# Token-major projections in blocks of 512 columns instead of 256

## The chip, the core and the metric

One core of a Trainium2 chip. The metric is device microseconds of one execution, from which a median over runs is taken. The engines that matter are TensorE (matmul, and transposes as matmuls against an identity), VectorE, ScalarE, GpSimd, and SyncE, which issues most DMA transfers. The profile calls them PE, DVE, ACT, POOL and SP.

## What is computed

Two transformer blocks on 256 tokens of width 1024, in float32. The first block is a gated FFN, a mixer of two attentions (low-rank with rope, and dilated), and a second FFN; the second block works on its output and on a context that the first block's stream also feeds, with three mixers (mLSTM scan, differential attention, state-space scan), a gated merge and a convolutional FFN.

```python
def hybrid_mixer(u, ...):
    proj = u @ w_in
    cq, ckv, kr, dq, dk, dv, g = jnp.split(proj, ...)
    q = (rms_norm(cq, q_norm_g) @ w_uq)
    c_kv = rms_norm(ckv, kv_norm_g)
    ...
    merged = gates[:, :, 0] * (o_a @ w_branch_a) + gates[:, :, 1] * (o_b @ w_branch_b)
    return merged @ w_out

def first_block(x, positions, ...):
    f1 = swiglu(rms_norm(h, ffn1_pre_g), ffn1_w_gate, ffn1_w_up, ffn1_w_down)
    h = h + 0.5 * rms_norm(f1, ffn1_post_g)
    mix = hybrid_mixer(rms_norm(h, mix_pre_g), ...)
    h = h + rms_norm(mix, mix_post_g)
    f2 = swiglu(rms_norm(h, ffn2_pre_g), ...)
    return h + 0.5 * rms_norm(f2, ffn2_post_g)
```

## The kernel before

**Layout and precision.** The 256 tokens are two blocks of 128 (TB = 2). A product in float32 is made of three matmuls on rounded halves (`mm3`, L353 to L358): high by high, high by low, low by high. Activations that feed a projection stand transposed, as eight k-rows of 128 features by 256 tokens, each in a high and a low half (`Split`). A feature-major projection (`proj_fm`, L370) has the weights stationary and 256 tokens moving. A token-major one (`proj_tm`, L380) has 128 tokens stationary and the weight columns moving, and it is this kind that the change is about: blocks of 256 columns (224 for `w_in_a`), one PSUM tile of one bank for both token blocks, outer loop over the token blocks, inner loop over the eight k-rows. `down` (L390) is token-major too, with 512 columns moving and four accumulators.

**The order of the work.** The kernel sets the order of instructions by hand. The engines take what is queued for them in program order and meet through semaphores. `tick(us)` (L197) is called after each stretch of TensorE work with an estimate of its length. It advances a clock of the program (a number at build time, no time of the chip), then steps the side chains that are marked first (evacuations, made by `later`), then calls `weights.ahead()`, then steps each other side chain that is due, once. A side chain is a generator: what stands between two of its yields is queued in one go, and a yield can name a wait in the program's clock. `join` runs a side chain to its end at once.

**Weights.** `Weights` (L94) streams all weights in the order of use, in loads of 512 KB: `load` issues the DMA on SyncE's queue, five raw tiles deep (NRAW). `split` (L116) makes the high half on ScalarE (L127) and the low half on VectorE (L128) into a ring of four (RING). With 256 columns a load holds four k-rows, so a block has two loads; with 512 it holds two k-rows, so a block has four; with 336 three, three and two. `take` (L143), at the head of a block, splits what of the block isn't split yet, and sets `now` to the block's first load. `ahead` (L138) splits on while fewer than four loads in the ring have a number of `now` or above; so the loads of a block count as used when the next block is taken.

**The stages that use `proj_tm`.** `ctx_attn` (L1206), run beside the residual norm behind the first FFN; `mixer1` (L756) for `w_in_a` and `w_in_b`; `ctx_mlstm` (L1225), beside the residual norm behind the first mixer; `mixer2` (L1473) for the mLSTM values and output gate, and for query, key and value of the differential attention. `residual_norm` (L445) is a side chain whose steps go from PSUM through VectorE (L457, L460, L478) to `to_T`, eight transposes for a token block (L512). `low_rank` (L740) normalises two slices of `w_in_a`'s result (L747) and transposes them (L752). `lat_scalars` (L1303) makes the gate scalars of the mLSTM and ends in transposes (L1348). `prep_a` (L1521), the query and key chain of the differential attention, is started inside the loop over six blocks, at the fifth.

**Modulation rows.** `mod_rows` (L940) multiplies 16 pieces of a matrix, loaded on ScalarE's queue (L972), on VectorE (L980), and adds them up over partitions on TensorE (L957). Each of its passes has 22 steps, and it is due by the program's clock at a fixed pace: 6.0 us a step for two passes during the first mixer and later, 2.0 us for four more (88 steps) that start at the first tick when the two are done. What of the four is left when the second FFN ends is run at the join there, with no other work beside it.

Of the kernel before, what the change touches and what calls it, by code (L numbers as in the profile page):

```python
# [16 lines left out]
D = 1024  # L17
# [18 lines left out]
SHAPES = {"f1_gu": (8, 256), "f1_dn": (2, D), "w_in_a": (8, 224), "w_in_b": (8, 256), "w_in_g": (8, 256), "w_uq_t": (3, 384),  # L36
          "w_ukv": (2, 1024), "w_br_a": (4, 256), "w_br_b": (4, 256), "w_out_t": (2, D), "f2_gu": (8, 256), "f2_dn": (2, D),
          "w_ctx": (8, 256), "w_rows": (8, 32), "w_lat": (8, 256), "w_br_m2": (4, 256), "w_br_a2": (4, 256),
# [3 lines left out]
def weight_order():  # L42
# [8 lines left out]
    add("w_ctx", 4, 5, 6, 7)  # L51
    add("w_in_a", 0, 1, 2)
    add("w_rows", 0)
    add("w_in_b", 4, 5, 0, 1)
    add("w_uq_t", 0, 1)
    add("w_ukv", 0)
    add("w_in_b", 2, 3)
# [5 lines left out]
    add("w_ctx", 2, 3, 0, 1)  # L63
    add("f2_gu", *range(NFF))
    add("f2_dn", *range(NFF // 2))
    add("w_ctx", 8, 9, 10)
    add("w_rows", 0)
    add("w_lat", *range(24))
    add("w_br_m2", 0, 1, 2, 3)
    add("w_lat", 24, 25, 26, 27)  # L70
    add("w_br_a2", 0, 1, 2, 3)
    add("w_lat", 28, 29, 30, 31)
# [110 lines left out]
class Net:  # L183
# [196 lines left out]
    def proj_tm(self, name, i, xT, ps):  # L380

        nk, cols = SHAPES[name]
        w = self.weights.take(name, i)
        p = ps([128, TB, cols])
        for tb in range(TB):
            self.tm_block(p[:, tb], w, xT, nk, tb, 0, cols)
            self.tick(nk * 0.327)
        return p
# [367 lines left out]
    def mixer1(self, xT, m):  # L756
# [449 lines left out]
    def ctx_attn(self, xT):  # L1206
# [18 lines left out]
    def ctx_mlstm(self, xT):  # L1225
# [39 lines left out]
    def ctx_ssd(self, xT):  # L1265
# [3 lines left out]
        for i in range(3):  # L1269
            p = self.proj_fm("w_ctx", 8 + i, xT, self.psA)  # L1270
# [202 lines left out]
    def mixer2(self, xT, aside):  # L1473
# [11 lines left out]
        def evac(p, i):  # L1485
            for tb in range(TB):
                nc.scalar.activation(va[tb][:, 2 * i:2 * i + 2, :128], p[:, tb].rearrange("p (h d) -> p h d", h=2), AF.Copy)

        for i in range(2):
            s2 = self.later(0, evac, self.proj_tm("w_lat", 4 + i, xT, B), i)  # L1490
# [4 lines left out]
        def evac(p, i):  # L1495
# [5 lines left out]
        for i in range(2):  # L1501
            s3 = self.later(0, evac, self.proj_tm("w_lat", 6 + i, xT, B), i)
# [105 lines left out]
        def evac(p, i):  # L1608
            nc.scalar.activation((qa, ka, vv)[i // 2][:, :, (i % 2) * 256:(i % 2) * 256 + 256], p, AF.Copy)
# [312 lines left out]
```

## Time and profile before

| | us |
|---|---|
| median of three runs | 1292.15 |
| lowest, highest | 1290.20, 1292.22 |
| the profiled execution | 1290.56 |
| its span, first to last instruction | 1288.8 |

The profile shows one execution. Its span is cut into 40 slices on the page, with the busy share of each engine in tenths and the TensorE clock that was granted; it has groups of instructions by source line, with the mean duration of one and the idle time before them, and who ended that. The trace behind it can be asked for single instructions (start, duration, engine, line, operation, operands, and in brackets how long the engine stood idle before and whose result ended that) and for the busy time in windows. A matmul's duration there reaches past the start of the next, since matmuls are pipelined: what one costs is read from start to start.

### The profile page before, as it was taken

How to read it: one execution, taken by the hardware profiler on the slowest of the kernel's cores; microseconds unless marked ns; L12 is line 12 of the kernel's file. 1: busy time of each engine (PE TensorE's matmuls, PEld its weight loads, DVE VectorE, ACT ScalarE, POOL GpSimd, SP SyncE). 2: the span in 40 equal slices, each digit the busy share in tenths (PEclk: the TensorE clock that was granted, in tenths of full speed). 3: DMA queues.
4: the chain of work that ended last, by engine and by line, in shares of the span. 5: the costliest groups of instructions: out<-in, count | busy, mean ns of one | idle time of the engine just before them, and what ended most of it. 6: DMA issues, size and time to landing. Idle time of an engine off the chain costs nothing. (4 is left out here: it accounts for less than half of the span.)

```text
span 1288.8 us, 22199 instructions
## 1 busy us (share of the span) xinstructions
PE 1199.3 (93%) x8728; PEld 1115.0 (87%) x8728; DVE 934.0 (72%) x1603; ACT 624.1 (48%) x1063; POOL 66.9 (5%) x84
## 2 busy tenths in 40 slices
PE   7999998999999999999981699999999998999998
PEld 7999977999878889999860599999888897999977
DVE  4897857667766786767857878589666767888854
ACT  4454545455564464444420454556465344555542
POOL 0020000100000000000000001035100000000000
PEclk8999999999999999999995799999999998999999
DMA  7878785666343766657896355345413265555562
GB/s 265 273 229 256 257 291 195 206 218 218 123 135 116 292 199 221 222 188 247 299 338 216 100 195 190 133 156 172 143 54 100 98 209 216 172 173 181 179 241 85
DMA packets 80605, 251.32 MB, mean 195 GB/s; under 512 B 9523, under 2 KB 10851, under 8 KB 80502
## 3 DMA queue, kind: packets, MB, share of 16 engines
q1 hardware_dynamic: 61654, 215.85, 49.6%
q10 hardware_dynamic: 18432, 33.56, 7.8%
q0 software_dynamic: 416, 0.50, 0.4%
q8 instruction: 68, 1.11, 0.3%
q14 instruction: 35, 0.29, 0.1%
HBM read 241.46 MB, written 8.42 MB: 194 GB/s over the span
## 5 line engine op out<-in xcount | busy, mean ns | idle before, releaser
L128 DVE TENSOR_TENSOR wl<-raw,wh 128x1024 fp32r<-128x1024 f32 (+3 forms) x358 | 424.1, 1218 | 137.0 <-ACT wh L127 133.8
L356 PE MATMUL pB<-u,wh 128*128 128x256 f32 x1696 | 486.6, 287 | 0.7 <-ACT u L347 0.7
L358 PE MATMUL pB<-u,wl 128*128 128x256 f32 x1696 | 481.9, 284 | 1.0 <-DVE wl L128 1.0
L357 PE MATMUL pB<-u,wh 128*128 128x256 f32 x1696 | 481.5, 284 | 0.6 <-DVE u L348 0.3
L127 ACT ACTIVATE wh<-raw 128x1024 fp32r<-128x1024 f32 (+3 forms) x358 | 359.3, 1045 | 93.1 <-PE pB L358 33.8
L356 PEld LDWEIGHTS pB<-u,wh 128*128 128x128 f32 x1696 | 326.0, 192 | 9.4 <-issue 6.8
L358 PEld LDWEIGHTS pB<-u,wl 128*128 128x128 f32 x1696 | 326.0, 192 | 2.3 <-DVE wl L128 1.4
L357 PEld LDWEIGHTS pB<-u,wh 128*128 128x128 f32 x1696 | 326.0, 192 | 1.8 <-DVE u L348 1.4
L356 PE MATMUL pB<-wh,u 128*128 128x512 f32 (+3 forms) x614 | 208.1, 339 | 1.7 <-ACT wh L127 1.7
L357 PE MATMUL pB<-wl,u 128*128 128x512 f32 (+3 forms) x614 | 207.6, 338 | 2.2 <-DVE wl L128 2.0
L358 PE MATMUL pB<-wh,u 128*128 128x512 f32 (+3 forms) x614 | 206.5, 336 | 0.0
L357 PEld LDWEIGHTS pB<-wl,u 128*128 128x128 f32 x614 | 117.0, 191 | 15.7 <-DVE wl L128 5.0
L356 PEld LDWEIGHTS pB<-wh,u 128*128 128x128 f32 x614 | 117.0, 191 | 14.1 <-ACT wh L127 2.4
L358 PEld LDWEIGHTS pB<-wh,u 128*128 128x128 f32 x614 | 117.0, 190 | 11.7
L428 POOL TENSOR_TENSOR rs<-ms,nhalf 128x1 f32<-128x1 f32 (+2 forms) x30 | 28.4, 946 | 877.2 <-DVE ms L422 874.5
L520 ACT ACTIVATE w<-pB 128x256 f32<-128x256 f32 x44 | 16.9, 383 | 116.7 <-PE pB L358 116.3
L980 DVE SCALAR_TENSOR_TENSOR v<-v,silu_c,v 128x512 f32<-128x512 f32 x84 | 62.8, 748 | 12.3 <-DMA v<-w_mod 11.2
L1006 DVE SCALAR_TENSOR_TENSOR w<-pB,cols,w 128x255 f32<-128x255 f32 x120 | 49.6, 476 | 15.8 <-ACT w L1001 10.1
L521 DVE SCALAR_TENSOR_TENSOR w<-w,pB 128x256 f32<-128x256 f32 x44 | 18.5, 420 | 50.2 <-ACT w L520 49.8
L957 PE MATMUL pA<-v,onesr 128*1 128x512 f32 x16 | 7.3, 456 | 42.5 <-ACT v L347 42.5
L356 PE MATMUL pA<-wh,u 128*128 128x256 f32 x132 | 38.5, 292 | 2.4 <-ACT u L347 1.7
L957 PEld LDWEIGHTS pA<-v,onesr 128*1 128x1 f32 x16 | 1.3, 83 | 45.2 <-ACT v L347 45.0
(365 smaller groups left out, 1421.9 us busy)
## 6 DMA issues: line engine op xcount, KB each, us to landing
raw<-f_gu SPq DMA_DIRECT2D x88, 512.0 KB
v<-w_mod ACTq DMA_DIRECT2D x128, 256.0 KB
raw<-w_lat SPq DMA_DIRECT2D x64, 512.0 KB
raw<-f_dn SPq DMA_DIRECT2D x44, 512.0 KB
raw<-w_up_t SPq DMA_DIRECT2D x44, 512.0 KB
raw<-w_ctx SPq DMA_DIRECT2D x22, 512.0 KB
raw<-w_down_t SPq DMA_DIRECT2D x22, 512.0 KB
raw<-w_in_g SPq DMA_DIRECT2D x16, 512.0 KB
```

What stands on the lines that cost most here:

```text
L127: nc.scalar.activation(hi, r, AF.Copy)
L128: nc.vector.tensor_tensor(out=lo, in0=r, in1=hi.bitcast(F32), op=OP.subtract)
L356: nc.tensor.matmul(out, a[0], b[0], start=first, stop=False)
L357: nc.tensor.matmul(out, a[0], b[1], start=False, stop=False)
L358: nc.tensor.matmul(out, a[1], b[0], start=False, stop=last)
L428: self.nc.gpsimd.tensor_tensor(out=r, in0=ms, in1=self.nhalf[:, :width], op=OP.pow)
L520: nc.scalar.activation(th, p[:, 0], AF.Tanh, scale=0.5)
L521: nc.vector.scalar_tensor_tensor(th, th, 1.0, p[:, 0], op0=OP.add, op1=OP.mult)
L957: nc.tensor.matmul(p[:1], self.onesr[:, :1], hi, start=True, stop=False)
L980: nc.vector.scalar_tensor_tensor(acc, ws[n - ahead], sc, acc, op0=OP.mult, op1=OP.add)
L1006: nc.vector.scalar_tensor_tensor(y[j][:, o], p[:, j, x], tap(t, i), y[j][:, o], op0=OP.mult, op1=OP.add)
```

## The change

The token-major projections get blocks of 512 columns (336 for `w_in_a`). The weights of `w_lat` and `w_ctx` are laid out anew, those that are used token-major in arrays of their own (`w_lat_t`, `w_ctx_t`), with the indices of the rest moved. In `proj_tm` the loop over k-rows is the outer one, the two token blocks are inside, each in a PSUM tile of its own. After the k-rows of one load, `W.now` moves past that load, so that it counts as used, and `tick` is called with 0.0026 us a row and column: 2.66 for two rows of 512. That is as many ticks as before for the same columns. Each evacuation works on a token block of 512 columns. `prep_a` starts behind the second of three blocks, after a join with that block's evacuation.

```diff
-SHAPES = {"f1_gu": (8, 256), "f1_dn": (2, D), "w_in_a": (8, 224), "w_in_b": (8, 256), "w_in_g": (8, 256), "w_uq_t": (3, 384),
+SHAPES = {"f1_gu": (8, 256), "f1_dn": (2, D), "w_in_a": (8, 336), "w_in_b": (8, 512), "w_in_g": (8, 256), "w_uq_t": (3, 384),
           "w_ukv": (2, 1024), "w_br_a": (4, 256), "w_br_b": (4, 256), "w_out_t": (2, D), "f2_gu": (8, 256), "f2_dn": (2, D),
-          "w_ctx": (8, 256), "w_rows": (8, 32), "w_lat": (8, 256), "w_br_m2": (4, 256), "w_br_a2": (4, 256),
+          "w_ctx": (8, 256), "w_ctx_t": (8, 512), "w_rows": (8, 32), "w_lat": (8, 256), "w_lat_t": (8, 512), "w_br_m2": (4, 256), "w_br_a2": (4, 256),
...
     def proj_tm(self, name, i, xT, ps):
 
         nk, cols = SHAPES[name]
-        w = self.weights.take(name, i)
-        p = ps([128, TB, cols])
-        for tb in range(TB):
-            self.tm_block(p[:, tb], w, xT, nk, tb, 0, cols)
-            self.tick(nk * 0.327)
+        W = self.weights
+        w = W.take(name, i)
+        a, per = W.now, W.items[W.now][3]
+        p = [ps([128, cols]) for _ in range(TB)]
+        for k in range(nk):
+            for tb in range(TB):
+                self.mm3(p[tb], tuple(t[:, tb * 128:tb * 128 + 128] for t in xT[k]), w(k, 0, cols), k == 0, k == nk - 1)
+            if k % per == per - 1 or k == nk - 1:
+                W.now = a + k // per + 1
+                self.tick((k % per + 1) * cols * 0.0026)
         return p
...
-                nc.scalar.activation(proj[tb][:, i * 224:(i + 1) * 224], p[:, tb], AF.Copy)
-
-        for i in range(3):
+                nc.scalar.activation(proj[tb][:, i * 336:(i + 1) * 336], p[tb], AF.Copy)
+
+        for i in range(2):
...
-        def evac(p, i, dst):
-            nc.scalar.activation(dst[:, :, (i % 2) * 256:(i % 2) * 256 + 256], p, AF.Copy)
+        def evac(p, dst):
+            for tb in range(TB):
+                nc.scalar.activation(dst[:, tb], p[tb], AF.Copy)
 
         dqk = [self.u([128, TB, 512]) for _ in range(2)]
-        for i, dst in ((4, dv), (5, dv), (0, dqk[0]), (1, dqk[0])):
-            s = self.later(0, evac, self.proj_tm("w_in_b", i, xT, B), i, dst)
+        for i, dst in ((2, dv), (0, dqk[0])):
+            s = self.later(0, evac, self.proj_tm("w_in_b", i, xT, B), dst)
...
-        for i in range(2, 4):
-            s = self.later(0, evac, self.proj_tm("w_in_b", i, xT, B), i, dqk[1])
-        self.join(s)
+        self.join(self.later(0, evac, self.proj_tm("w_in_b", 1, xT, B), dqk[1]))
...
-            nc.scalar.activation((ka, va)[i // 2][:, :, (i % 2) * 256:(i % 2) * 256 + 256], p, AF.Copy)
-
-        for i in range(4):
-            s = self.later(0, evac, self.proj_tm("w_ctx", 4 + i, xT, self.psA), i)
+            for tb in range(TB):
+                nc.scalar.activation((ka, va)[i][:, tb], p[tb], AF.Copy)
+
+        for i in range(2):
+            s = self.later(0, evac, self.proj_tm("w_ctx_t", 1 + i, xT, self.psA), i)
...
+        def evac(p):
             for tb in range(TB):
-                nc.scalar.activation(va[tb][:, 2 * i:2 * i + 2, :128], p[:, tb].rearrange("p (h d) -> p h d", h=2), AF.Copy)
-
-        for i in range(2):
-            s = self.later(0, evac, self.proj_tm("w_ctx", 2 + i, xT, self.psA), i)
+                nc.scalar.activation(va[tb][:, :, :128], p[tb].rearrange("p (h d) -> p h d", h=4), AF.Copy)
+
+        self.later(0, evac, self.proj_tm("w_ctx_t", 0, xT, self.psA))
         kp = self.u([128, 4, T])
         for i in range(2):
...
+        s2 = self.later(0, evac, self.proj_tm("w_lat_t", 0, xT, B))
 
         og = self.u([128, TB, 512])
         mg = self.bcast("m_norm_g_2", 512)
 
-        def evac(p, i):
-            c = slice(i * 256, i * 256 + 256)
-            th = self.v([128, TB, 256])
-            nc.scalar.activation(th, p, AF.Tanh, scale=0.5)
-            nc.vector.scalar_tensor_tensor(og[:, :, c], th, 1.0, mg[:, None, c].to_broadcast([128, TB, 256]), op0=OP.add, op1=OP.mult)
-
-        for i in range(2):
-            s3 = self.later(0, evac, self.proj_tm("w_lat", 6 + i, xT, B), i)
+        def evac(p):
+            for tb in range(TB):
+                th = self.v([128, 512])
+                nc.scalar.activation(th, p[tb], AF.Tanh, scale=0.5)
+                nc.vector.scalar_tensor_tensor(og[:, tb], th, 1.0, mg, op0=OP.add, op1=OP.mult)
+
+        s3 = self.later(0, evac, self.proj_tm("w_lat_t", 1, xT, B))
...
-            nc.scalar.activation((qa, ka, vv)[i // 2][:, :, (i % 2) * 256:(i % 2) * 256 + 256], p, AF.Copy)
-
-        for i in range(6):
-            s = self.later(0, evac, self.proj_tm("w_lat", 8 + i, xT, B), i)
-            if i == 4:
+            for tb in range(TB):
+                nc.scalar.activation((qa, ka, vv)[i][:, tb], p[tb], AF.Copy)
+
+        for i in range(3):
+            s = self.later(0, evac, self.proj_tm("w_lat_t", 2 + i, xT, B), i)
+            if i == 1:
+                self.join(s)
                 self.side(prep_a())
```

## Rows read from the trace of the kernel before

**Rows 1.** Part 1 of the page: engine, busy us (share of the span), instructions.

```profile
PE 1199.3 (93%) x8728; PEld 1115.0 (87%) x8728; DVE 934.0 (72%) x1603; ACT 624.1 (48%) x1063; POOL 66.9 (5%) x84
```

**Rows 2.** Windows by stage; columns in the first line, then one stage each.

```profile
core 0: us, PE busy (x) PEld busy (x) DVE busy (x) ACT busy (x) POOL busy (x), PEclk, DMA share, GB/s
...
205.00:241.00 36.00, 32.04 (x235) 30.37 (x234) 25.78 (x37) 18.32 (x34) 2.19 (x4) 0.95 0.49 158
241.00:290.00 49.00, 49.00 (x411) 48.63 (x410) 29.24 (x51) 25.50 (x48) 5.39 (x7) 1.00 0.74 240
...
446.00:475.00 29.00, 26.08 (x201) 24.91 (x200) 23.76 (x41) 18.35 (x37) 2.19 (x4) 0.94 0.61 205
...
671.00:721.00 50.00, 6.85 (x16) 1.51 (x15) 35.98 (x53) 4.30 (x9) 0.00 (x0) 0.53 0.65 214
...
806.00:856.00 50.00, 48.31 (x386) 47.08 (x387) 36.12 (x99) 28.37 (x57) 1.21 (x2) 1.00 0.41 139
```

**Rows 3.** Timeline, TensorE, in three projections: start, duration, line, tile, shape, count.

```profile
203.04 0.39 PE L356 MATMUL pB<-wh,u 128*128 128x512 f32 x1
...
208.71 0.39 PE L357 MATMUL pB<-wl,u 128*128 128x512 f32 x1
...
226.43 0.28 PE L357 MATMUL pA<-wl,u 128*128 128x256 f32 x1
...
231.47 0.28 PE L357 MATMUL pA<-wl,u 128*128 128x256 f32 x1
...
245.79 0.28 PE L358 MATMUL pB<-wh,u 128*128 128x224 f32 x1
...
249.92 0.28 PE L356 MATMUL pB<-wh,u 128*128 128x224 f32 x1
```

**Rows 4.** Groups by line and form: count | busy us, mean ns | idle before.

```profile
L128 DVE TENSOR_TENSOR wl<-raw,wh 128x1024 fp32r<-128x1024 f32 x346 | 414.2, 1231 | 125.8 <-ACT wh L127 122.7
...
L127 ACT ACTIVATE wh<-raw 128x1024 fp32r<-128x1024 f32 x346 | 350.8, 1055 | 93.1 <-PE pB L358 33.8 <-PE pA L358 25.5 <-DMA raw<-f_dn 8.8
```

**Rows 5.** Timeline, TensorE: first transposes of a norm; in brackets the wait before.

```profile
224.80 1.32 PE L512 MATMUL pB<-ident,u 128*128 128x128 f32 x8 [1.51 <-DVE u L478]
...
459.72 1.32 PE L512 MATMUL pB<-ident,u 128*128 128x128 f32 x8 [1.13 <-DVE u L478]
```

**Rows 6.** Timeline, VectorE, ahead of the second of these.

```profile
453.17 2.36 DVE L128 TENSOR_TENSOR wl<-raw,wh 128x1024 fp32r<-128x1024 f32 x2 [0.57 <-ACT wh L127]
...
455.52 1.28 DVE L457 TENSOR_TENSOR u<-pB,u 128x512 f32<-128x512 f32 x2
...
458.92 1.41 DVE L478 SCALAR_TENSOR_TENSOR u<-u,rs,u 128x512 f32<-128x512 f32 x2
```

**Rows 7.** Timeline, ScalarE, VectorE and TensorE, low-rank chain and rope, first mixer.

```profile
259.33 2.96 ACT L127 ACTIVATE wh<-raw 128x1024 fp32r<-128x1024 f32 x3
...
266.52 0.48 DVE L747 SCALAR_TENSOR_TENSOR u<-u,rs,u 128x256 f32<-128x256 f32 x1 [0.73 <-POOL rs L428]
...
270.00 0.71 PE L752 MATMUL pA<-ident,u 128*128 128x128 f32 x5
...
306.65 1.05 PE L829 MATMUL pA<-ident,u 128*96 128x128 f32 x8 [0.37 <-DVE u L690]
```

**Rows 8.** Timeline, TensorE, behind the second FFN: two results one pass apart.

```profile
692.10 0.58 PE L957 MATMUL pA<-v,onesr 128*1 128x512 f32 x1 [9.54 <-ACT v L347]
...
711.75 0.59 PE L957 MATMUL pA<-v,onesr 128*1 128x512 f32 x1 [9.86 <-ACT v L347]
```

**Rows 9.** Timeline, ScalarE and TensorE, gate scalars and first heads, second mixer.

```profile
804.40 0.42 ACT L1341 ACTIVATE w<-w 64x256 f32<-64x256 f32 x1 [1.59 <-DVE w L1340]
...
805.66 0.27 PE L1348 MATMUL pA<-ident,w 64*128 64x64 f32 x1
...
825.95 0.49 PE L1378 MATMUL pA<-vx,v 128*128 128x129 f32 x2 [0.74 <-DVE nd L1384]
...
828.70 0.44 PE L1090 MATMUL pA<-rbs,pick 128*128 128x384 f32 x1 [0.95 <-DVE nd L1384]
```

More of the change, by code (lines that the diff above doesn't have):

```diff
@@ L50, in weight_order @@
     add("f1_dn", *range(NFF // 2))
-    add("w_ctx", 4, 5, 6, 7)
-    add("w_in_a", 0, 1, 2)
+    add("w_ctx_t", 1, 2)
+    add("w_in_a", 0, 1)
     add("w_rows", 0)
-    add("w_in_b", 4, 5, 0, 1)
+    add("w_in_b", 2, 0)
     add("w_uq_t", 0, 1)
     add("w_ukv", 0)
-    add("w_in_b", 2, 3)
+    add("w_in_b", 1)
     add("w_in_g", 0, 1, 2, 3, 4, 5)
@@ L62, in weight_order @@
     add("w_out_t", 0, 1, 2, 3)
-    add("w_ctx", 2, 3, 0, 1)
+    add("w_ctx_t", 0)
+    add("w_ctx", 0, 1)
     add("f2_gu", *range(NFF))
     add("f2_dn", *range(NFF // 2))
-    add("w_ctx", 8, 9, 10)
+    add("w_ctx", 2, 3, 4)
     add("w_rows", 0)
-    add("w_lat", *range(24))
+    add("w_lat", 0, 1, 2, 3)
+    add("w_lat_t", 0, 1, 2, 3, 4)
+    add("w_lat", *range(4, 14))
     add("w_br_m2", 0, 1, 2, 3)
-    add("w_lat", 24, 25, 26, 27)
+    add("w_lat", 14, 15, 16, 17)
     add("w_br_a2", 0, 1, 2, 3)
-    add("w_lat", 28, 29, 30, 31)
+    add("w_lat", 18, 19, 20, 21)
     add("w_br_s2", 0, 1, 2, 3)
@@ L1269, in ctx_ssd @@
         for i in range(3):
-            p = self.proj_fm("w_ctx", 8 + i, xT, self.psA)
+            p = self.proj_fm("w_ctx", 2 + i, xT, self.psA)
             s = self.side(self.conv_silu(p, self.col["s_conv_w"], self.col["s_conv_b"], 2 * i, 8, [xb[i][:, j] for j in range(2)]), first=True)
@@ L1483, in mixer2, with evac @@
         va = [self.vx() for _ in range(TB)]
-        def evac(p, i):
+        def evac(p):
             for tb in range(TB):
-                nc.scalar.activation(va[tb][:, 2 * i:2 * i + 2, :128], p[:, tb].rearrange("p (h d) -> p h d", h=2), AF.Copy)
-        for i in range(2):
-            s2 = self.later(0, evac, self.proj_tm("w_lat", 4 + i, xT, B), i)
+                nc.scalar.activation(va[tb][:, :, :128], p[tb].rearrange("p (h d) -> p h d", h=4), AF.Copy)
+        s2 = self.later(0, evac, self.proj_tm("w_lat_t", 0, xT, B))
         og = self.u([128, TB, 512])
         mg = self.bcast("m_norm_g_2", 512)
-        def evac(p, i):
-            c = slice(i * 256, i * 256 + 256)
-            th = self.v([128, TB, 256])
-            nc.scalar.activation(th, p, AF.Tanh, scale=0.5)
-            nc.vector.scalar_tensor_tensor(og[:, :, c], th, 1.0, mg[:, None, c].to_broadcast([128, TB, 256]), op0=OP.add, op1=OP.mult)
-        for i in range(2):
-            s3 = self.later(0, evac, self.proj_tm("w_lat", 6 + i, xT, B), i)
+        def evac(p):
+            for tb in range(TB):
[3 more added lines that the diff above has]
+        s3 = self.later(0, evac, self.proj_tm("w_lat_t", 1, xT, B))
         self.join(s, s2, s3)
@@ L1617, in mixer2 @@
         for i in range(4):
-            p = self.proj_fm("w_lat", 14 + i, xT, B)
+            p = self.proj_fm("w_lat", 4 + i, xT, B)
             s = self.side(self.conv_silu(p, self.col["s_conv_w"], self.col["s_conv_b"], 2 * i, 8, [xbc[i][:, j] for j in range(2)]), first=True)
@@ L1627, in mixer2 @@
         for i in range(2):
-            s2 = self.later(0, evac, self.proj_fm("w_lat", 18 + i, xT, B), i)
+            s2 = self.later(0, evac, self.proj_fm("w_lat", 8 + i, xT, B), i)
         self.join(s, s2)
@@ L1631, in mixer2 @@
         m = [self.u([128, 4, T]) for _ in range(2)]
-        for n, i in (("m", 20), ("a", 24), ("s", 28)):
+        for n, i in (("m", 10), ("a", 14), ("s", 18)):
             g = self.gates("w_lat", range(i, i + 4), None, xT)
@@ L1814, in pack_first @@
         o[f"f{f}_dn"] = tiles_rows(x[f"ffn{f}_w_down"][0])
-    o["w_in_a"] = tiles_k(w[:, :672], 224)
-    o["w_in_b"] = tiles_k(w[:, 672:2208], 256)
+    o["w_in_a"] = tiles_k(w[:, :672], 336)
+    o["w_in_b"] = tiles_k(w[:, 672:2208], 512)
     o["w_in_g"] = tiles_k(w[:, 2208:], 256)
@@ L1862, in pack_second @@
     o["w_rows"] = tiles_k(rows, 32)
-    o["w_lat"] = tiles_k(np.concatenate([qk, v, og, aq, ak, av, xbc, z, gates], axis=1), 256)
-    o["w_ctx"] = tiles_k(np.concatenate([qk[:, 512:], v, ak, av, xbc[:, :768]], axis=1), 256)
+    o["w_lat"] = tiles_k(np.concatenate([qk, xbc, z, gates], axis=1), 256)
+    o["w_lat_t"] = tiles_k(np.concatenate([v, og, aq, ak, av], axis=1), 512)
+    o["w_ctx"] = tiles_k(np.concatenate([qk[:, 512:], xbc[:, :768]], axis=1), 256)
+    o["w_ctx_t"] = tiles_k(np.concatenate([v, ak, av], axis=1), 512)
     for n in "mas":
```

## The prediction, made before the change was run

> **What bounds the kernel now.** I read the busy shares first [rows 1]: TensorE's matmuls fill 1199.3 of 1288.8 us, VectorE 934.0, ScalarE 624.1. So the time is TensorE's work plus the some 90 us in which it waits, and a change counts only if it shortens TensorE's stream or moves one of its waits. The table by stage comes second [rows 2]: in the first mixer (241 to 290) TensorE is busy for all of 49.00 us, so its own pace is the bound; in the two stages in which a residual norm runs beside context projections (205 to 241, 446 to 475) it lacks 3.96 and 2.92 us; in 806 to 856 it lacks 1.69; and in 671 to 721 it is busy 6.85 of 50 us. Third, the timeline of TensorE gives the pace of its matmuls [rows 3], and the bracketed waits give what holds it where it stands still [rows 5, 7, 8, 9]: a VectorE or ScalarE result each time, never a transfer, in the stages the change touches. The readers of this kernel should therefore look at two things: how many ns a matmul column costs, and in which order VectorE and ScalarE, which take their instructions as the program queued them, get the weight splits and everything else.
>
> **The change part by part.**
>
> *Wider matmuls.* From start to start, 256 columns go by at (231.47 − 226.43)/42 = 120 ns, 512 at (208.71 − 203.04)/25 = 227 ns and 224 at (249.92 − 245.79)/37 = 111.6 ns [rows 3]. The 512 rows come from the down projection, which has the same roles as the new loop: activations stationary, weights moving. One matmul of 512 in the place of two of 256 saves 2 × 120 − 227 = 13 ns. There are eleven blocks of 512 after the change (context 3, first mixer 3, second mixer 5), each of 8 × 2 × 3 = 48 matmuls: 528 × 13 = 6.9 us. For the block of 336 the line between 256 and 512 gives 120 + 80/256 × 107 = 153.4 ns; 144 × 111.6 − 96 × 153.4 = 16.07 − 14.73 = 1.3 us. Together −8.2 us, if TensorE is what everything waits for.
>
> The skill has a rule that speaks against this: the Trainium skill, "TensorE: Matmul & The Clock Gate", section "Back-to-back issue gap", gives a warm gap of N/2.4 + 2.5 ns, so 109.2 for 256 and 215.8 for 512, and a merged pair would save 2.6 ns; here 120 and 227 are measured, 11 ns more for each instruction, and it is that surplus that merging removes.
>
> *Evacuations, PSUM, DMA.* A pair of blocks of 256 was emptied by two or four ScalarE instructions, a block of 512 by two; the elements are the same. A block now holds two PSUM banks of four for 48 × 0.227 = 10.9 us, where a bank was held for 48 × 0.120 = 5.8 of a rotation of 23: the next use comes after 21.8 us, far behind any evacuation. The loads keep their size, number and queue order on SyncE. I cost all this at nothing; the cover is TensorE's own pace.
>
> *Each load freed on its own.* A load's split is 1.055 us on ScalarE and 1.231 on VectorE [rows 4]; queued back to back they take 1.0 and 1.18 (2.96 for three on ScalarE [rows 7], 2.36 for two on VectorE [rows 6]). Before, the two loads of a block were split as a pair at the tick in its middle, into slots that TensorE had left half a block (2.88 us) earlier, so ScalarE and VectorE ran ahead of TensorE. After, one split is queued at each load's tick, into the slot of the very load TensorE has just worked on. ScalarE's copy has to wait until TensorE has finished it, and every step of a side chain queued at that tick sits behind it on ScalarE, then on VectorE: 1.06 + 1.23 = 2.3 us after TensorE's end of the load. The next tick's TensorE work comes 12 × 0.227 = 2.7 us after it. A chain step that used to be in time by less than 2.3 us is now late. Also, the first block of 512 needs all four loads split before it is queued, where 256 needed two. Place by place:
>
> - *Context attention* (205 to 241). The first transposes of the residual norm already wait 1.51 us for VectorE's normalisation, at 224.80 [rows 5]. With one more split (1.18) ahead of that on VectorE they start at about 225.95. Half of the stage's gain, 48 × 13 = 0.6, lies in front of this gate and is eaten by a longer wait. Loss 1.15 + 0.6 = 1.8; bounds 0.6 (the split lands behind the step) and 3.0 (two splits ahead).
> - *Context mLSTM* (446 to 475). The same gate waits 1.13 at 459.72 [rows 5]. VectorE's order in front of it is two splits, then the norm's multiplications [rows 6]; the block of 512 puts two more splits there: 2.36 us, start about 462.05. The stage's own gain of 0.6 lies in front and is lost with it. Loss 3.0; bounds 0.6 and 3.0.
> - *First mixer.* Today nothing waits there except 0.37 at 306.65 [rows 7]. The low-rank chain passes ScalarE behind three splits (259.33 to 262.29), ends on VectorE at 267.00, and its transposes on TensorE start at 270.00 without a wait: 3 us to spare, less what the split order adds at each crossing of ScalarE and VectorE. Three such chains (transposes of the context keys, low rank, rope of the first half of the heads) I put at 0.6, 0.7 and 1.2 in full: 2.5. The lower bound is 0, since the rows show no wait.
> - *Second mixer.* The gate scalars cross DVE, ACT, DVE, ACT and reach TensorE's transposes at 805.66 without a wait; the last ScalarE step that those need runs from 804.40 to 804.82 [rows 9], so some 0.9 us is to spare. Up to three single splits can come in between, 3 × 1.18 − 0.9 = 2.6. The mLSTM heads already wait 0.74 at 825.95 and 0.95 at 828.70 [rows 9]; there and in the heads behind it I add 1.4, as much again as two such waits; the key and query chain of the attention starts two ticks earlier, which I take to give back one of them, 0.7. In full 3.3, lower bound 0.
>
> For these last two, 5.8 in full and 0 as the rows stand, I take half, 2.9: the nearest rows are ones without a wait, but with spare time of the order of one split.
>
> *The program's clock.* The side that makes the modulation rows runs by the program's clock, a step each 2.0 us, and starts at the first tick after 264 us from the start of the first mixer. The ticks now add up to 125.1 instead of 126.3 in that mixer (w_in_a −1.7, w_in_b +0.6) and 21.1 instead of 20.9 in the mLSTM stage. So the second FFN starts at 161.8 instead of 162.8, tick 39 behind it falls at 263.865, just short of 264, and the side starts one tick later, while the join ends at 328.9 instead of 329.9. That leaves 33 steps done of 88, not 34. The rest runs in the hole at 671 to 721, where nothing covers it. A pass of 16 loads takes 711.75 − 692.10 = 19.65 us [rows 8], 1.2 us a step. Loss 1.2; bounds 0 and 1.4.
>
> *Sum.* −8.2 + 1.8 + 3.0 + 2.9 + 1.2 = +0.7 us. The profiled execution took 1290.56 (span 1288.8), 1.6 under the median of 1292.15, and becomes 1291.3; on the median that is 1292.9.
>
> **Rivals.**
>
> *The slack covers the splits (faster).* If ScalarE and VectorE are ahead of TensorE by over 2.3 us wherever a chain needs them, no wait grows, and only the extra step of the clock is paid: −8.2 + 1.2 = −7.0, 1285.2. For it: TensorE is busy all of 241 to 290 and VectorE only 29.24 of 49.00 us there, ScalarE 25.50 [rows 2]; and a load freed early lets its successor be split early. Against: both gates [rows 5] are bound by VectorE already, and the splits are put ahead of them.
>
> *Single splits hold up TensorE in the mixers too (slower).* Place: the chains from ScalarE and VectorE to TensorE's transposes at 254 to 310 and 800 to 830. Price: the full 5.8 instead of 2.9, so +3.6, 1295.8. It decides once the time to spare at those transposes is under one split's 2.3 us; the 0.9 us at 805.66 [rows 9] speaks for it, the 3 us at 270.00 [rows 7] against. A bound beyond it: the granted clock averages 0.95 and 0.94 in the two context stages [rows 2], so about 0.05 × 36/0.5 = 3.6 us of each run at 1.2 GHz. TensorE stands still there before the fall. A longer stand at a gate may cause another such stretch, 1.8 us each: up to 1299.4.
>
> *The pitch doesn't fall.* If the new loop, which changes PSUM bank after every three matmuls, keeps the surplus of a column and saves only some 2.6 ns a pair, the gain is 1.4 and not 8.2: 1299.7. The down projection changes banks in the same way at 227 ns [rows 3], so little is left for this.
>
> **How the numbers follow.** Forecast 1292.9 (own range 1290 to 1296): 0.40. Covered, 1285.2: 0.26. Held up, 1295.8 to 1299.4: 0.28. Pitch, 1299.7: 0.03. Something else, on the slower side: 0.03. A measurement of this kernel can tell about 0.2%, 2.6 us, so same is 1289.6 to 1294.7. Faster: all but 0.01 of the covered case and 0.03 of the forecast, 0.28. Same: 0.31 of the forecast, 0.01 covered, 0.02 held up, 0.34. Slower: 0.06 + 0.26 + 0.03 + 0.03 = 0.38. The range from 1285 to 1300 leaves out the far part of the covered case and little above.
>
> **What would show it.** Matmuls of 512 at 227 ns and of 336 near 153 in the projections; single splits on VectorE, where pairs of 2.36 us stood; the transposes of the first norm step at about 226 and 462 less what was gained in front; waits of 0.5 to 2.5 us at the low-rank, rope and gate-scalar transposes; the hole behind the second FFN longer by about 1.2 us. I am wrong if the gates don't move, if the mixers' TensorE stays as full as 49.00 of 49.00, or if the hole keeps its length.

## The result: 1.05% slower

The changed kernel takes 1306.0 us in the median where the kernel before takes 1292.2: the ratio is 1.0105, with a 95% interval of 1.0083 to 1.0127. Forecast were 1292.9 us and a range up to 1300. One of the four runs behind the median took 1628.8 us at a granted clock of 0.68 and isn't in the ratio; the median of the other three is 1304.6. The profile shown here is of an execution of the changed kernel that took 1305.1 us (span 1303.1); it answers to one of 1290.56 (span 1288.8) before. So 14.3 us of span have to be found.

Part 1 of its page, which answers to [rows 1]:

```profile
PE 1200.2 (92%) x8152; PEld 1090.6 (84%) x8152; DVE 935.2 (72%) x1603; ACT 624.8 (48%) x1057; POOL 69.2 (5%) x84
```

There are 576 matmuls fewer than before (8152 for 8728), 528 from the blocks of 512 and 48 from the block of 336. Yet TensorE is busy for as long as before (in part at a lower clock, as shown below), and ScalarE and VectorE do the same work. The windows by stage, which answer to [rows 2], each moved to where the stage now lies:

```profile
core 0: us, PE busy (x) PEld busy (x) DVE busy (x) ACT busy (x) POOL busy (x), PEclk, DMA share, GB/s
205.00:245.00 40.00, 32.69 (x141) 26.05 (x140) 27.27 (x38) 19.53 (x35) 2.20 (x4) 0.91 0.48 149
245.00:294.00 49.00, 48.06 (x272) 43.28 (x271) 28.90 (x50) 27.26 (x48) 5.94 (x7) 1.00 0.76 255
455.00:492.00 37.00, 29.37 (x193) 26.38 (x193) 26.68 (x46) 20.36 (x36) 2.51 (x3) 0.91 0.53 170
678.50:726.60 48.10, 6.08 (x13) 1.01 (x11) 35.75 (x51) 4.25 (x9) 0.00 (x0) 0.54 0.67 220
812.00:865.00 53.00, 48.09 (x260) 40.89 (x261) 35.81 (x101) 28.43 (x58) 4.05 (x2) 1.00 0.37 121
```

The context attention window (first) lacks 7.3 us of TensorE where it lacked 4.0, at a granted clock of 0.91 for 0.95. The first mixer, filled to 49.00 of 49.00 before, lacks 0.9; the context mLSTM window (third) lacks 7.6, at 0.91 for 0.94; the last window, in the second mixer, lacks 4.9 of 53. The hole behind the second FFN (fourth) is no longer than before.

A sharper view goes by the weights, which both kernels use in the same order: the time from the first matmul of one weight block to the first matmul of another is the length of a stage. Before, and what each kernel of this study adds to it, in us, from one profiled execution each (the experiments follow below; the first and last rows, in which nothing is changed, show how far such a difference strays by itself, up to 2). The columns are, in this order, the changed kernel and the runs called narrow_release, late_release, late_release_prep, change_prep_split_last and mixers_late_prep below:

| stage | before | change | narrow, release | late release | late release, prep | change, prep, split last | mixers, late, prep |
|---|---|---|---|---|---|---|---|
| up to the context projections | 211.9 | +0.4 | +1.5 | +2.1 | +1.0 | +1.0 | +0.3 |
| context attention | 29.3 | +3.5 | +3.2 | +2.1 | +2.0 | +2.2 | 0.0 |
| w_in_a, w_in_b 2 and 0 | 44.3 | -1.2 | +1.2 | -2.4 | -2.4 | -2.4 | -2.4 |
| up to the end of w_in_b 1 | 30.5 | +1.1 | +2.0 | -0.2 | -0.2 | -0.2 | -0.2 |
| rest of the first mixer, w_out | 130.2 | -0.4 | 0.0 | -0.6 | -0.6 | -0.6 | -0.6 |
| context mLSTM | 36.1 | +6.0 | +4.8 | +4.0 | +4.3 | +2.0 | +1.9 |
| second FFN and hole | 238.4 | -3.3 | -2.0 | -2.8 | -3.2 | -3.3 | -2.2 |
| context SSD, start of second mixer | 56.9 | -0.1 | 0.0 | 0.0 | 0.0 | 0.0 | 0.0 |
| wide blocks of the second mixer | 78.2 | +2.3 | +7.5 | -3.2 | -3.2 | -3.2 | -3.2 |
| rest of the second mixer | 240.5 | +5.9 | 0.0 | +4.2 | -0.4 | -0.4 | +0.2 |
| last FFN | 188.8 | +0.2 | -1.3 | -1.3 | +1.5 | -1.4 | +0.2 |

The column of the change holds the gain (the -1.2 in the first mixer is what is left of 2.4) and its losses: the two context stages, a first one in the first mixer (+1.1), the wide blocks of the second mixer, and, unforeseen, the rest of that mixer.

**The pace of the matmuls**, which answers to [rows 3], from TensorE's timeline:

```profile
238.54 0.39 PE L360 MATMUL pA<-wl,u 128*128 128x512 f32 x1
...
242.62 0.39 PE L360 MATMUL pA<-wl,u 128*128 128x512 f32 x1
...
251.44 0.32 PE L361 MATMUL pB<-wh,u 128*128 128x336 f32 x1
...
254.82 0.32 PE L359 MATMUL pB<-wh,u 128*128 128x336 f32 x1
```

18 matmuls of 512 lie between the first two rows, 4.08/18 = 227 ns, and 22 of 336 between the last two, 3.38/22 = 153.6 ns, as forecast.

**The gates of the two residual norms**, which answer to [rows 5]:

```profile
226.31 0.90 PE L520 MATMUL pB<-ident,u 128*128 128x128 f32 x3 [4.73 <-DVE u L486]
...
465.23 1.12 PE L520 MATMUL pB<-ident,u 128*128 128x128 f32 x4 [4.71 <-DVE u L486]
```

They wait 4.73 and 4.71 us, where they waited 1.51 and 1.13. What VectorE has in front of them is as forecast. In front of the first gate, before:

```profile
219.37 1.23 DVE L128 TENSOR_TENSOR wl<-raw,wh 128x1024 fp32r<-128x1024 f32 x1 [0.60 <-ACT wh L127]
```

In the changed kernel two splits stand in that place, and in front of the second gate four, where there were two [rows 6]:

```profile
219.76 2.36 DVE L131 TENSOR_TENSOR wl<-raw,wh 128x1024 fp32r<-128x1024 f32 x2 [0.60 <-ACT wh L130]
...
456.41 3.50 DVE L131 TENSOR_TENSOR wl<-raw,wh 128x1024 fp32r<-128x1024 f32 x3 [0.57 <-ACT wh L130]
...
463.29 1.22 DVE L131 TENSOR_TENSOR wl<-raw,wh 128x1024 fp32r<-128x1024 f32 x1
```

Two windows of the kernel before, and then two of the changed one, show what came with that (PEclk is the granted clock):

```profile
core 0: us, PE busy (x) PEld busy (x) DVE busy (x) ACT busy (x) POOL busy (x), PEclk, DMA share, GB/s
...
213.00:217.00 4.00, 3.85 (x19) 3.85 (x20) 3.34 (x8) 0.94 (x4) 0.55 (x1) 0.57 0.90 319
...
225.00:232.00 7.00, 6.99 (x59) 6.75 (x58) 5.77 (x10) 4.73 (x7) 0.55 (x1) 1.00 0.23 68
```

The changed kernel, the same columns:

```profile
226.30:233.00 6.70, 6.69 (x23) 5.67 (x24) 3.29 (x6) 2.46 (x5) 0.55 (x1) 0.60 0.26 77
465.20:472.00 6.80, 6.77 (x25) 5.84 (x26) 3.31 (x6) 1.50 (x3) 1.42 (x1) 0.60 0.49 155
```

Before, the stretch at half clock (0.57) lies in front of the first gate, and the gate's wait swallows it. After, TensorE stands 4.73 us at the gate, and the 6.7 us behind it are granted 0.60 in the mean, where before they had 1.00: 6.7 x (1 - 0.60) = 2.7 us, and nothing swallows them. The same follows the second gate: 6.8 x (1 - 0.60) = 2.7.

**The queue order** can be read off the second transposes of the first norm, on ScalarE, VectorE and TensorE together:

```profile
232.72 1.06 ACT L130 ACTIVATE wh<-raw 128x1024 fp32r<-128x1024 f32 x1 [3.82 <-PE pA L361]
233.69 1.06 ACT L1220 ACTIVATE u<-pA 128x512 f32<-128x512 f32 x2
233.82 1.23 DVE L131 TENSOR_TENSOR wl<-raw,wh 128x1024 fp32r<-128x1024 f32 x1 [4.04 <-ACT wh L130]
234.96 1.41 DVE L486 SCALAR_TENSOR_TENSOR u<-u,rs,u 128x512 f32<-128x512 f32 x2
...
235.76 1.32 PE L520 MATMUL pB<-ident,u 128*128 128x128 f32 x8 [0.35 <-DVE u L486]
```

ScalarE's split at 232.72 has stood 3.82 us, until TensorE's last matmul on the load whose slot it takes (L361). VectorE's half of it stood 4.04 us, until ScalarE was done. The norm's step (L486), whose last operand GpSimd had finished at 227.9, comes off VectorE's queue only behind it, and TensorE's transposes (L520) wait for that, here 0.35 us. The Trainium skill, "Perfetto Trace Analysis", section "Per-engine timelines", says that ScalarE, VectorE and GpSimd are strict FIFO; these rows agree.

**The waits in the mixers**, which answer to [rows 7] and [rows 9]:

```profile
259.28 0.55 PE L942 MATMUL pA<-ident,u 128*128 128x128 f32 x3 [0.94 <-DVE u L1127]
...
310.47 1.05 PE L838 MATMUL pA<-ident,u 128*96 128x128 f32 x8 [1.82 <-DVE u L698]
...
813.19 0.33 PE L1356 MATMUL pA<-ident,w 128*128 128x128 f32 x1 [2.49 <-ACT w L1348]
```

The transposes of the context keys wait 0.94 (before, none), those of the rope 1.82 (0.37), those of the gate scalars 2.49 (none). The low-rank transposes (270.00 before) still don't wait. **The hole**, which answers to [rows 8]:

```profile
698.94 0.58 PE L964 MATMUL pA<-v,onesr 128*1 128x512 f32 x1 [10.07 <-ACT v L350]
...
717.79 0.58 PE L964 MATMUL pA<-v,onesr 128*1 128x512 f32 x1 [9.06 <-ACT v L350]
```

A pass takes 18.85 us for 19.65 before, and the hole is 48.1 us long where it was 49.3.

### The profile page after: what moved, and what is told of

It is laid out like the page before. It is cut to its first block, busy times and chain, and to the rows that moved or that the text cites. A ratio compares the mean times of both kernels' runs of the same rounds, so it can differ in the third digit from the quotient of the medians.

```text
span 1626.8 us, 21054 instructions
## 1 busy us (share of the span) xinstructions
PE 1561.6 (96%) x8152; PEld 1332.0 (82%) x8152; DVE 938.8 (58%) x1603; ACT 629.0 (39%) x1057; POOL 62.1 (4%) x84
## 3 DMA queue, kind: packets, MB, share of 16 engines
q8 instruction: 64, 1.05, 0.3%
## 4 chain that ended last, share of the span: by engine, by line
PE 92%; DVE 4%; DMA 2%; ACT 1%; issue 1%; ACTq 0%; SPq 0%; POOL 0%; DVEq 0%; POOLq 0%
PE pB L359 25%; PE pB L360 25%; PE pB L361 25%; PE pA L360 2%; PE pA L359 2%; PE pA L361 2%; DVE v L987 1%; DMA v<-w_mod 1%; PE pA L745 1%; PE pB L520 1%; PE pB L738 1%; PE pA L852 1%; PE pB L1473 1%; PE pB L1475 1%; DVE wl L131 1%
## 5 line engine op out<-in xcount | busy, mean ns | idle before, releaser
L359 PE MATMUL pB<-u,wh 128*128 128x256 f32 x1696 | 570.0, 336 | 0.0
L360 PE MATMUL pB<-u,wh 128*128 128x256 f32 x1696 | 564.4, 333 | 0.3
L361 PE MATMUL pB<-u,wl 128*128 128x256 f32 x1696 | 563.6, 332 | 0.0
L359 PEld LDWEIGHTS pB<-u,wh 128*128 128x128 f32 x1696 | 406.8, 240 | 13.5 <-issue 12.1
L360 PEld LDWEIGHTS pB<-u,wh 128*128 128x128 f32 x1696 | 407.7, 240 | 2.2 <-DVE u L351 0.9
L361 PEld LDWEIGHTS pB<-u,wl 128*128 128x128 f32 x1696 | 408.9, 241 | 0.0
L359 PE MATMUL pB<-wh,u 128*128 128x512 f32 (+2 forms) x470 | 230.7, 491 | 0.0
L360 PE MATMUL pB<-wl,u 128*128 128x512 f32 (+2 forms) x470 | 230.1, 490 | 0.0
L361 PE MATMUL pB<-wh,u 128*128 128x512 f32 (+2 forms) x470 | 229.3, 488 | 0.0
L361 PEld LDWEIGHTS pB<-wh,u 128*128 128x128 f32 x470 | 97.5, 207 | 47.5 <-issue 12.3
L359 PEld LDWEIGHTS pB<-wh,u 128*128 128x128 f32 x470 | 97.8, 208 | 45.4 <-issue 12.8
L360 PEld LDWEIGHTS pB<-wl,u 128*128 128x128 f32 x470 | 97.3, 207 | 44.8 <-issue 12.4
L528 ACT ACTIVATE w<-pB 128x256 f32<-128x256 f32 x44 | 16.9, 384 | 204.0 <-PE pB L361 204.0
L1013 DVE SCALAR_TENSOR_TENSOR w<-pB,cols,w 128x255 f32<-128x255 f32 x120 | 49.6, 476 | 44.0 <-ACT w L1008 29.3
L436 POOL TENSOR_TENSOR rs<-ms,nhalf 128x1 f32<-128x1 f32 (+2 forms) x30 | 27.4, 912 | 1138.3 <-DVE ms L430 1135.6
L359 PE MATMUL pA<-u,wh 128*128 128x256 f32 (+2 forms) x112 | 39.3, 351 | 0.0
L360 PE MATMUL pA<-u,wh 128*128 128x256 f32 (+2 forms) x112 | 38.7, 346 | 0.0
```

The lines of the kernel that those rows point to most:

```text
L359: nc.tensor.matmul(out, a[0], b[0], start=first, stop=False)
L360: nc.tensor.matmul(out, a[0], b[1], start=False, stop=False)
L361: nc.tensor.matmul(out, a[1], b[0], start=False, stop=last)
L436: self.nc.gpsimd.tensor_tensor(out=r, in0=ms, in1=self.nhalf[:, :width], op=OP.pow)
L528: nc.scalar.activation(th, p[:, 0], AF.Tanh, scale=0.5)
L1013: nc.vector.scalar_tensor_tensor(y[j][:, o], p[:, j, x], tap(t, i), y[j][:, o], op0=OP.mult, op1=OP.add)
```

## The experiments

Two theories stood at first: S, that the release of each load costs the time, because its split goes into the slot that TensorE has just left and side steps stand in the queue behind it; and D, that a block of four loads in a ring of four costs it, however the loads are freed. A third, C, blamed the program's clock. Ratios are against runs of the kernel before on the same chip.

**The changed kernel again** (no edit), for the profile above.

> The changed kernel once more, for a profile at the full granted clock. All theories: 1303 to 1308 us. Theory S (the release of each load: one split is queued at each tick, into the slot of the load that TensorE has just used, so ScalarE and VectorE fall behind): in the projections the matmuls start 227 ns apart (512) and about 153 ns apart (336), VectorE's weight splits stand alone, and TensorE waits 1 to 3 us several times in each mixer. Theory D (the block of four loads in a ring of four: all four have to be split before a block can be queued, whatever the release): the waits stand at the heads of the blocks, for the block's own splits. Theory C (the program's clock): the hole behind the second FFN is longer by several us.

Measured: 1304.6 us, ratio 1.0107 (1.0091 to 1.0124). The waits are those of S. The hole is not longer, so C falls.

**Loop order and release of the change, with 256 columns.** Against before:

```diff
     def proj_tm(self, name, i, xT, ps):
-        p = ps([128, TB, cols])
-        for tb in range(TB):
-            self.tm_block(p[:, tb], w, xT, nk, tb, 0, cols)
-            self.tick(nk * 0.327)
+        p = [ps([128, cols]) for _ in range(TB)]
+        for k in range(nk):
+            for tb in range(TB):
+                self.mm3(p[tb], ...)
+            if k % per == per - 1 or k == nk - 1:
+                W.now = a + k // per + 1
+                self.tick(nk * 0.327)
```

> Before with the loop order and the release of the change, but blocks of 256 (224) columns: k-rows outside, token blocks inside in two PSUM tiles, a load counted as used and the clock called after its rows, the calls of the clock with the old 2.616 us. Theory S: the release is what costs; the loss of the change without its gain, 1302 to 1314 us. Theory D: a block of two loads in a ring of four leaves room, 1291 to 1295 us.

Measured: 1307.0 us, ratio 1.0119 (1.0092 to 1.0147). S holds and D falls: with blocks of two loads and the clock of before, the loss is there, 16.9 us by the table, and none of it in the rest of the second mixer, where the changed kernel loses 5.9. The two largest waits of TensorE in the first mixer, and the largest one in the second, by what they waited for (total, times, longest):

```profile
PE pA L835 <- DVE u L695: 1.6, 1, 1.6
PE pA L941 <- DVE u L1126: 0.9, 1, 0.9
...
PE pA L1356 <- ACT w L1348: 2.3, 1, 2.3
```

They stand at the same places as in the change: the rope (1.6), the context keys (0.9), the gate scalars (2.3).

**The same without the release.**

```diff
-                W.now = a + k // per + 1
                 self.tick(nk * 0.327)
```

> The same as narrow_release without the release: loads count as used when the next block is taken, as before; loop order and two PSUM tiles of the change stay. Both S and D: the order of the queues is that of before, 1291 to 1295 us. A loss here would put the cost on the loop order or the doubled number of evacuations.

Measured: 1291.1 us, ratio 1.0007 (0.9989 to 1.0025). One line decides over 15.9 us. Neither the loop order nor the doubled number of evacuations costs anything that can be seen, to some 0.2%.

**The change with each load freed one load later.**

```diff
-                W.now = a + k // per + 1
+                W.now = a + k // per
                 self.tick((k % per + 1) * cols * 0.0026)
```

> The changed kernel with each load counted as used one load later, so that a split goes into a slot that TensorE left a whole load (2.7 us) before. Theory S: most of the loss is gone, 1288 to 1298 us. Theory D: a block has one load less in hand when it is taken, 1303 to 1312 us.

Measured: 1291.9 us, ratio 1.0007 (0.9992 to 1.0021): 12.8 us are back, as S says. ScalarE's splits show it. From the groups by line and form (count, busy us, mean ns, idle time before and who ended it), the change:

```profile
L130 ACT ACTIVATE wh<-raw 128x1024 fp32r<-128x1024 f32 x346 | 352.5, 1055 | 136.3 <-PE pB L361 68.1 <-PE pA L361 32.6 <-DMA raw<-f_dn 9.8
```

The same group of the late release:

```profile
L130 ACT ACTIVATE wh<-raw 128x1024 fp32r<-128x1024 f32 x346 | 352.5, 1055 | 102.4 <-PE pB L361 45.6 <-PE pA L361 25.3 <-DMA raw<-f_dn 7.7
```

Their idle time falls from 136.3 to 102.4 us; before the change it was 93.1 [rows 4]. Still there is no gain over before, though the wide blocks of the second mixer are 3.2 us shorter now: 4.2 are lost in the rest of that mixer, and 6 in the context stages.

**The query and key chain two ticks later.** Two kernels, with the late release and with the change's own:

```diff
-                self.side(prep_a())
+                self.side(prep_a(), 5.5)
```

> late_release, and the query and key chain of the differential attention (prep_a) starts two ticks later, where it started before. In late_release the stretch behind the last of the second mixer's wide blocks is 4.3 us longer than before; TensorE waits 3.4 us there for GpSimd at the chain's transposes, before 0.5. Theory P (the early start queues those transposes on TensorE before GpSimd's rope is done): 1287 to 1289 us, the wait back at about 0.5. Rival Q (the wait comes from the release or the blocks' width, whenever the chain starts): 1291 to 1293 us.

> The changed kernel, its release as it is, with prep_a started two ticks later. Theory P: 3 to 4.5 us under the changed kernel, 1300 to 1302 us. Q: 1304 to 1306 us.

Measured: 1286.9 us, ratio 0.9957 (0.9939 to 0.9975), and 1300.2 us, ratio 1.0059 (1.0036 to 1.0082): 0.50% and 0.48% less than without the edit. The rest of the second mixer is shorter by 4.6 us with the late release and by 5.0 with the change's own. P holds and Q falls. Of the 4.6 us 2.9 are TensorE's waits for GpSimd, and a wait of 1.4 us for VectorE (L1601), which the kernel before doesn't have, goes too. TensorE's waits for GpSimd in the stretch around the chain's transposes (total, times, longest), in the late release:

```profile
PE pA L942 <- POOL u L1138: 3.4, 2, 2.6
```

And with the later start:

```profile
PE pA L942 <- POOL u L1138: 0.5, 1, 0.5
```

Where it comes from stands on GpSimd's timeline of the late release:

```profile
858.97 1.95 POOL L436 TENSOR_TENSOR rs<-ms,nhalf 128x4 f32<-128x4 f32 x1 [3.47 <-DVE ms L430]
860.89 2.97 POOL L1136 TENSOR_TENSOR w<-u,rot 128x256 f32<-128x256 f32 x4
...
872.02 0.91 POOL L1138 TENSOR_TENSOR u<-w,w 128x256 f32<-128x256 f32 x1
...
903.67 1.70 POOL L1138 TENSOR_TENSOR u<-w,w 128x256 f32<-128x256 f32 x1
```

and on TensorE's:

```profile
871.87 0.27 PE L942 MATMUL pA<-ident,u 128*128 128x128 f32 x1
872.99 0.55 PE L942 MATMUL pA<-ident,u 128*128 128x128 f32 x3 [0.84 <-POOL u L1138]
...
905.42 0.55 PE L942 MATMUL pA<-ident,u 128*128 128x128 f32 x3 [2.55 <-POOL u L1138]
```

The rope (from L1136) can start only at 860.89, behind a power of another chain (L436) for which GpSimd had to wait, and it ends at 872.93. TensorE, which takes the chain's transposes by the program's clock, had them in front at 871.87. The rope of the queries ends at 905.37, and there TensorE waits the other 2.55 us.

**Wide blocks in the mixers alone.** late_release_prep, with `w_ctx` back in blocks of 256 and the loop of before for them (the functions `ctx_attn`, `ctx_mlstm` and `ctx_ssd` are those of before):

```diff
     def proj_tm(self, name, i, xT, ps):
         nk, cols = SHAPES[name]
+        if cols <= 256:
+            return self.proj_tm_old(name, i, xT, ps)
```

> late_release_prep with the three context projections that run beside the residual norms back in blocks of 256 columns as before (loop, release and clock too); the mixers keep the wide blocks. Theory G (a block of four loads puts one or two more splits ahead of the norm chain on VectorE, and TensorE stands at the chain's first transposes): the two stages are back at their lengths of before, 3 to 6 us under late_release_prep, 1282 to 1286 us. Rival (those stages vary by themselves, by the stretches at half clock): within 1 us of late_release_prep.

Measured: 1284.3 us, ratio 0.9935 (0.9916 to 0.9954). That is 0.22% or 2.8 us under late_release_prep (the means of their own runs differ by 3.2, give or take 2.0), at the lower edge of the 3 to 6 that G expects. The gate of the context attention waits 1.50 us again, and the stage has its length of before (0.0 in the table):

```profile
225.06 1.10 PE L531 MATMUL pB<-ident,u 128*128 128x128 f32 x6 [1.50 <-DVE u L497]
```

In the context mLSTM stage 1.9 of 4.3 us stay lost: TensorE stands 2.26 us at that gate, where it stood 1.13, and the 3.2 us behind it (456.9 to 460.1) run at 0.50, 1.6 us. The 0.0 of the other stage is in part luck. The next kernel, mixers_later_prep, has that stage queued in the same order, and it is 1.5 us longer in its profile: the stretch at half clock lies behind the gate there, with a stand of 3.01 us, and not in front. So the rival, that these stages vary by themselves, holds for a part, and how the 2.8 us divide isn't shown.

**Two loads later instead of one.**

```diff
-                W.now = a + k // per
+                W.now = max(a, a + k // per - 1)
```

> mixers_late_prep with each load counted as used two loads later instead of one. Theory S: what matters is that a split's slot was left by TensorE a whole load before; one load does it, and a second changes the time by less than 1.5 us. Rival (the earlier a load is freed, the better, as long as ScalarE doesn't wait): 1.5 us and more above mixers_late_prep, from two splits in a row at the head of each block.

Measured: 1287.2 us, ratio 0.9960 (0.9943 to 0.9977), 0.25% (3.2 us) above mixers_late_prep. That speaks for the rival and against S's "within 1.5 us". The means of their runs differ by 2.7 us, give or take 1.8: that it is slower is clear, that it is so by more than 1.5 isn't, and 1.5 is the context attention of its profile, told above.

**The split behind the side chains.** This one leaves the release as the change has it, and with it each split's slot and tick. Only the split's place in the queue moves: behind the steps of all side chains that the tick queues. Against change_prep:

```diff
     def ahead(self):
-        while self.nsplit < len(self.items) and ...:
+        while not self.hold and self.nsplit < len(self.items) and ...:
...
                 W.now = a + k // per + 1
+                W.hold = True
                 self.tick((k % per + 1) * cols * 0.0026)
+                W.hold = False
+                W.ahead()
```

> change_prep (1300.2 us, each load freed at once) with one thing moved: at the ticks inside a token-major projection the split is queued behind the steps of all side chains, not between the evacuations and the other chains. The same split goes into the same slot, at the same tick. Theory S1 (the loss is that side steps on ScalarE and VectorE stand in the queue behind a split that waits for TensorE): most of the 12 us between change_prep and late_release_prep come back, 1287 to 1293 us, and the 2.5 us at the gate scalars and 1.8 at the rope shrink. Rival S2 (the split itself is late for TensorE, wherever it stands): no better than 1298 us, with waits of TensorE for the weights' halves.

> mixers_late_prep (1284.3 us), but each load freed at once as in the change, and the split queued behind the side chains' steps at those ticks. S1: within 2 us of mixers_late_prep, 1283 to 1286 us. S2: 1288 us and more.

Measured: 1286.1 us, ratio 0.9963 (0.9940 to 0.9986), where change_prep has 1.0059; and 1284.5 us, ratio 0.9933 (0.9910 to 0.9957), where mixers_late_prep has 0.9935. S1 holds and S2 falls; the first is even a little under S1's 1287 to 1293. It is not the early slot that costs, nor a late split, but what stands behind the split. Of change_prep_split_last, the group of ScalarE's splits:

```profile
L131 ACT ACTIVATE wh<-raw 128x1024 fp32r<-128x1024 f32 x346 | 352.5, 1055 | 105.6 <-PE pB L362 40.4 <-PE pA L362 24.9 <-DMA raw<-f_dn 8.5
```

and the transposes of rope and gate scalars on TensorE's timeline:

```profile
307.45 1.05 PE L842 MATMUL pA<-ident,u 128*96 128x128 f32 x8 [0.68 <-DVE u L702]
...
803.31 0.33 PE L1360 MATMUL pA<-ident,w 128*128 128x128 f32 x1
```

The splits' idle time is 105.6 us, near the late release's. The rope waits 0.68 for 1.82, the gate scalars not at all.

**The same with 256 columns.** narrow_release, with the split queued last in the same way.

> narrow_release (1307.0 us: 256 columns, loop order and release of the change) with the split queued behind the side chains' steps at the ticks of the token-major projections. S1: the whole loss of narrow_release was the place in the queue, 1289 to 1293 us; then width alone is worth the difference to the wide kernels with the same queue order. S2: 1300 us and more.

Measured: 1294.1 us, ratio 1.0024 (1.0005 to 1.0043). Of narrow_release's 1.19% loss 0.95 are gone. The rest is in the context stages (+2.8 and +4.0 in its profile, with +1.3 in the rest of the second mixer; the stages with `proj_tm` in both mixers are at -0.1 to -0.6); it is just above the 1293 that S1 allowed. Between it and change_prep_split_last, equal in queue order, lies 0.61% or 7.9 us (the means of their runs differ by 8.2, give or take 2.6), which is what width is worth (with the program's clock and prep_a's place as each kernel has them).

Best of all are mixers_late_prep and mixers_split_last, with a ratio of 0.9935 and 0.9933: 0.65% faster than the kernel before, and 1.7% faster than the changed one.

## Why the prediction was wrong, step by step

The sum of the forecast was +0.7 us, and the span grew by 14.3. Three steps failed on the one side: the gates' losses "1.8" and "3.0" were 4.8 and 6.6 (6.6 us missing), "I take half", 2.9 for the mixers, was 7.9 (5.0 missing), and `prep_a`, credited with 0.7 in full, cost 5.0. On the other side the program's clock didn't cost 1.2, and the second FFN with the hole came out 3.3 shorter. In detail:

- **Wider matmuls: right.** Forecast -8.2 us; the pace is 227 and 153.6 ns. Where no wait eats it, the gain is there stage by stage: -3.2 in the second mixer's wide blocks (240 x 13 ns = 3.1), -2.4 in the first mixer's first ones (1.3 + 1.25). The width is worth 7.9 us between two kernels of equal queue order. The gap of N/2.4 + 2.5 ns of the Trainium skill, "TensorE: Matmul & The Clock Gate", section "Back-to-back issue gap", which the page gives for an isolated matmul, isn't seen here: these rows have 227 ns where it gives 215.8.
- **The gates: the queue order right, the loss too small.** The first starts at 226.31, and the stage began 0.4 later: 1.1 us more than before, for 1.15 forecast. The second is at 465.23, with the stage begun 3.3 us later: 2.2 more, for 2.33 forecast (one and two splits of 1.18). The failed step is "loss 1.8" and "loss 3.0": the term took the gate alone, with the stretch at half clock as a bound of 1.8 us further out. Measured are stages longer by 3.5 and 6.0, and with the gain of 1.25 and 0.6 that the sum counts elsewhere, losses of 4.8 and 6.6. The longer stand was followed by a stretch at half clock behind the gate, 2.7 us each time, where no wait covers it, and the old stretch in front of the gate had cost nothing. For the first stage 1.1 for the gate, 2.7 for the clock and 0.35 for the second transposes, less the gain of 0.6 behind the gate, make 3.6 of 3.5; for the second 2.2, 2.7 and 0.7 make 5.6 of 6.0. That the clock follows from the stand is argued from these rows; no run here changed the stand alone. It also strays: change_prep, queued alike up to there, stood 3.33 us at the first gate, lost 1.7 behind it, and its stage was 2.8 longer.
- **The mixers: the failed step is "I take half".** In full the terms were 2.5 and 3.3 us. From the change to the late release, 2.4 us come back in the first mixer up to the end of w_in_b 1 (1.2 + 1.3), and 5.5 in the wide blocks of the second, more than the 4.0 that the step had in full there without its credit for `prep_a`. The price of one split at each crossing was right at 2.49 for the gate scalars (2.6) and 1.45 for the rope (1.2), 0.94 at the context keys (0.6), 0 at the low-rank chain (0.7). The waits in the mLSTM heads, put at 1.4 more, went from 1.7 to 3.7 us in all, and are 1.2 with the late release. A row without a wait wasn't evidence for half; its spare time was known, and the sum in full followed from it.
- **prep_a: the wrong sign.** I credited 0.7 us for a chain that starts two ticks earlier. It cost 5.0 us in the changed kernel and 4.6 with the late release. The step looked at TensorE's waits for VectorE and passed over GpSimd's queue, through which this chain runs, and where its rope alone takes 12 us (860.89 to 872.93). Among the rows that the prediction rests on there was none of GpSimd's own timeline.
- **The program's clock: +1.2 not found.** The count itself holds: by the two kernels' own clock 54 of the 88 steps are left at the join before, and 55 after. But the hole is 1.2 us shorter, and the second FFN with it 3.3. The hole is from 46.8 to 49.6 us long over the twelve profiled executions of this study, so one step of 1.2 us can't be told in it. A kernel with the queue order of before (narrow_old_release) shows a hole of 48.3 us and 1.3 us less in that stage too, so part of this is spread between executions. The rest, some 2 us of gain, stays open.
- **The rival** "single splits hold up TensorE in the mixers too", at 0.28, was the case that came true. Its 1299.4 fell short because it had 1.8 us of clock for each gate where 2.7 were lost, 4.0 for the wide blocks of the second mixer where 5.5 were, and nothing for prep_a, which cost 5.0. The sum as it went, from the table: -1.2 + 1.1 - 0.4 + 2.3 in the mixers with the gain in it, 3.5 + 6.0 in the context stages, 5.9 in the rest of the second mixer, -3.3 for FFN and hole, 0.5 elsewhere: 14.4.

## What to carry to other kernels

Where engines take their work in order, ask of each instruction that waits for TensorE what is queued behind it: a buffer freed at once, and not one step later, gave nothing here and cost 12 us where its refill was queued ahead of the steps TensorE waits for. Queue such a refill last in its round, or free its buffer one step later; either gave the time back here. And when a chain is moved in a hand-written order, count every engine that it passes through, the slow one first.

## What the runs showed of the hardware

A stand of TensorE of 4.7 us at a gate was followed, twice, by 6.7 and 6.8 us at a mean granted clock of 0.60, 2.7 us lost each; before, with stands of 1.5 and 1.1 us, nothing was lost behind those gates.

Over the twelve profiled executions of this study the same holds: behind each of the 18 gates of the two residual norms with a stand of 2.2 to 4.7 us there is a stretch at 0.50 that loses 1.6 to 3.0 us, and behind the five with 1.1 to 1.5 us there is none. This doesn't show the stand to be the cause. All five short ones have such a stretch in front of the gate, which slows the work there and makes the stand shorter (the first gate stood 4.73 us in the changed kernel, and 3.33 in change_prep, which has one in front), and so have only seven of the 18. And the same queue order gave either: the first gate stood 1.50 us in mixers_late_prep, with the stretch in front and the stage as long as before, and 3.01 us in mixers_later_prep, with the stretch behind and 1.5 us more. A difference of 1 or 2 us between two profiled executions of such a stage is no evidence by itself.
